# Second feed-forward block: gate row multiplied into all down weights, down sums added by DVE alone, four PSUM banks

## The chip, the cores and the metric

The kernel runs on one core of a Trainium2 chip. The metric is the device time of one execution in microseconds (us); the median of three runs of the kernel before is 2130.88 us (2127.46 to 2131.03). The five engines are named as in the profile: PE (TensorE, matrix products; PEld is its loading of weights), DVE (VectorE), ACT (ScalarE), POOL (GpSimd) and SP (SyncE, which here issues most DMAs).

## The reference, cut to what matters

The reference is a network of two layers on 512 latent tokens and 256 context tokens of 1024 features, all in float32. Each layer has a mixer and a gated feed-forward block, each followed by a layer norm. The change is in the feed-forward block of the second (last) layer, where only the 512 latent tokens are left:

```
def conv_ffn(h, rows, w_gate, w_up, w_conv, w_down):
    a = h @ w_gate
    a = dwconv2d_centred(a.reshape(bt, rows, lt // rows, D_FF), w_conv).reshape(bt, lt, D_FF)
    return (jax.nn.silu(a) * (h @ w_up)) @ w_down

x = layer_norm(DEEP_ALPHA * x + g_f * conv_ffn(hf, ...), ln_g[li, 1], ln_b[li, 1])
```

`D_FF` is 2816. `g_f` is the gate row: one factor for each of the 1024 output features, the same for all tokens. It multiplies the result of the down product, feature by feature, so multiplying each column of `w_down` by its factor gives the same sum.

## The kernel before, in words

Every float32 product is made from three products of halves: weights and activations are each split into a high part (`whi`, `hh`, rounded by a cast on ACT) and a low part (`wlo`, `hl`, the rest, by a subtraction on DVE or POOL; `split`, L139 to L148), and PE adds high times high, high times low and low times high in PSUM. All products go through line 115.

`ffn` (from L1362) is called once for each layer; `l` is the layer, and `key` is None in the second. The 2816 hidden features are taken in 11 steps `p` of 256. In each step `gate_up(p)` (L1407) loads two weight units of 1 MB (gate and up, L1409), splits them, and for each half of 128 features makes the products with gate (`g_ps`) and up (`u_ps`), 24 products of 512 columns each. ACT and DVE then make the 3x3 convolution from the gate sums (L1431, eight steps at L1442), the silu (L1453), the product with up (L1454) and the split into `hh` and `hl` (L1457).

One step later the down products of that hidden pair follow (L1482 to L1488). `unit_rows` (L190) loads 256 rows of the down weights (1 MB, L194), multiplies them by a row if one is given (two multiplications on POOL of 128x1024, L197), and splits them in four parts. For each of the four token tiles and each half of the 1024 output columns, `down` (L1379) makes six products into one PSUM bank (`d_ps`), DVE multiplies the sum by the gate row into `gt` (L1391), and `gt` is added to the running sum `acc` of the tile: by POOL for the first half of the columns, by DVE for the second (L1488). So a down block is 48 products in eight groups. The down sums of the loop have two PSUM banks (L1376); gate and up have two each. Nine units of down weights are used in the loop. The last two (L1494) get the gate row multiplied into the weights already, and their products come in the tail (L1500 to L1523) with four more banks (`dp2`, L1503); there DVE adds the bank straight to `acc`, and the layer norm and the output follow.

The raw weights pass through two buffers (`raw`, L281): a unit's DMA is issued by SP when the split of the unit two before it is done. The split halves of the second layer pass through four pairs of buffers (L1402), in the order down, gate, up of each step. The gate row is loaded in front of the loop (`gate_rows`, L1189; its addition on POOL is L1198). The running sums are scaled at L1471 (DVE) and get a bias row at L1491 (POOL).

The order of instructions on each engine is laid down when the program is built, by a planner that follows the order of the code and fills waits that it foresees with later work; so some gate products of the next step stand between the groups of a down block in the trace. `pin` (L150) keeps an instruction behind all that its engine was given so far.

Of the kernel before, what the change touches and what calls it, by code (L numbers as in the profile page):

```python
# [20 lines left out]
P = 128  # L21
# [76 lines left out]
class Net:  # L98
# [22 lines left out]
    def rsqrt(self, pool, x, n, mul, add, tag):  # L121
        """(x*mul + add)^-0.5 on [128, n] float32, by three Newton steps (each flips the sign) to full precision."""
        v = self.nc.vector
        hv = pool.tile([P, n], F32, tag=tag + "h", name="rs_h")
        y = pool.tile([P, n], F32, tag=tag + "y", name="rs_y")
        w = pool.tile([P, n], F32, tag=tag + "w", name="rs_w")
        v.tensor_scalar(out=hv, in0=x, scalar1=0.5 * mul, scalar2=0.5 * add, op0=ALU.mult, op1=ALU.add)
        v.tensor_scalar(out=y.bitcast(I32), in0=hv.bitcast(I32), scalar1=-0.5, scalar2=MAGIC,
                        op0=ALU.mult, op1=ALU.add)
        for _ in range(3):  # L130
            if n == 1:
                v.scalar_tensor_tensor(out=w, in0=y, scalar=hv[:, 0:1], in1=y, op0=ALU.mult, op1=ALU.mult)
            else:
                v.tensor_mul(w, y, y)
                v.tensor_mul(w, w, hv)
            v.scalar_tensor_tensor(out=y, in0=w, scalar=1.5, in1=y, op0=ALU.subtract, op1=ALU.mult)
        return y
# [12 lines left out]
    def pin(self, ins):  # L150
        """Queue an instruction behind all that its engine was given so far."""
        return self.tc.keep_in_program_order(ins)

    @contextmanager
    def priority(self, offset):
        """Emit with a priority shifted by offset (positive: later)."""
        tc = self.tc
        old = tc.cur_priority
        tc.cur_priority = max(0, old + offset)
        start = tc.cur_priority  # L160
        try:
            yield
        finally:
            tc.cur_priority = old + (tc.cur_priority - start)

    def hilo(self):
        """The two split halves of the next weight unit, from the open weight pools in turn."""
        ps = self.wps
        pool = ps[self.wcount % len(ps)]
        self.wcount += 1  # L170
        return (pool.tile([P, 8 * 256], F32R, tag="whi", name="whi"),
                pool.tile([P, 8 * 256], F32R, tag="wlo", name="wlo"))

    def unit(self, parts, scale=None):
        """Load weight columns (list of [1024, w] DRAM blocks), scaled if asked for, and split them: [128, 8, 256]."""
# [14 lines left out]
    def unit_rows(self, src, scale=None):  # L190
        """Load [256, 1024] weight rows, with columns scaled if given, and split them: [128, 2, 1024]."""
# [10 lines left out]
    def proj_fm_g(self, w, c0, dsts):  # L202
        """Feature-major products: dsts = [(psum [128, n], t0, n)]; weights stationary."""
        wh, wl = w
        xh, xl = self.hT
        for k in range(KT):
            for wi, xi, first, last in ((wh, xh, True, False), (wh, xl, False, False), (wl, xh, False, True)):
                for ps, t0, n in dsts:
                    self.mm(ps, wi[:, k, c0:c0 + P], xi[:, k, t0:t0 + n],
                            start=(k == 0 and first), stop=(k == KT - 1 and last))  # L210
                    yield n // 256

    def proj_tm_g(self, ps, w, t, c0=0, n=256):
        """Token-major products for token tile t; activations stationary."""
# [19 lines left out]
    def set_work(self, items, side=None):  # L234
        """items: [(weight parts, generator function of the loaded unit)], run in order by tick()."""
# [13 lines left out]
    def _step(self):  # L249
        """Advance the current item; its cost, or None at its end."""  # L250
# [19 lines left out]
    def drain(self, upto):  # L270
        """Run until the first `upto` items are complete."""
# [39 lines left out]
    def rows_T(self, pool, psp, src, n, dst, doff=0):  # L311
        """DRAM rows [n, 128] -> dst[:, doff:doff+n] (transposed)."""
# [7 lines left out]
    def cond(self, pool, psp):  # L320
        """silu(c), silu(c_ctx) as a zero-padded stationary operand [128, 8, 32]."""
# [22 lines left out]
    def mod_bias(self, pool, psp, l):  # L344
        """mod_b of layer l, per feature: [128, 48]."""
# [8 lines left out]
    def mod_group_g(self, mp, psp, l, g, tag="tr", bufs=2):  # L354
        """adaLN columns [2048 g, 2048 (g+1)) of layer l, both conditionings."""
# [30 lines left out]
    def h_params(self, key, lnidx, l, sub):  # L386
        """Scale/bias per feature of h = modulate(layer_norm(.)): from xhat."""
# [13 lines left out]
    def start(self, p2, w_in):  # L401
        """hT of layer 0, by pairs of feature tiles as the adaLN columns come in; q, k, v of delta heads."""
# [138 lines left out]
    def conv_evac(self, acc, blk, dst):  # L541
        """Three-tap convolution along the tokens of each stream, silu."""
# [120 lines left out]
    def fill_unit(self, fillp, pj, w, kind, i):  # L663
        """A 256-column block of the input projection, token-major, kept in DRAM."""
# [21 lines left out]
    def ab_load(self, w_in):  # L686
        """Columns 1792..2063: z of heads 2, 3 and the 16 decay / beta columns (one 272-column product)."""
# [13 lines left out]
    def ab_unit(self, dc, w_in):  # L701
# [5 lines left out]
        if True:  # L707
# [14 lines left out]
            # beta = 1 / (1 + exp(-b))  # L722
            nc.vector.tensor_scalar_add(be, e[:, 8:16], 1.0)
            nc.vector.reciprocal(be, be)
            # log1p(e) = 2 atanh(e / (2 + e))
# [17 lines left out]
        # decay columns: inclusive prefix, rest of the chunk, whole chunk  # L743
# [11 lines left out]
    def delta_head(self, h, hd, p1, p2):  # L755
# [3 lines left out]
        # norms  # L759
# [15 lines left out]
        bw = p2.tile([P, 2, 2, NT], F32, tag="bw", name="bw")  # (b, b * rest decay) x direction  # L775
# [6 lines left out]
        # decay matrices (transposed: row j, column i), products, U and P^T  # L782
# [38 lines left out]
    def delta_inverse(self, U, p1):  # L821
        """U_s = M_s^T, triangular, becomes ((I + M_s)^-1)^T: 16 x 16 by substitution, then block doubling."""
# [15 lines left out]
        # the 16 x 16 diagonal blocks, one per partition, each as a lower triangle: M (d = 0), M^T (d = 1)  # L838
# [29 lines left out]
        # 16 -> 32  # L868
# [16 lines left out]
        # 32 -> 64  # L885
# [37 lines left out]
        # 64 -> 128  # L923
# [19 lines left out]
    def delta_chain(self, h, hd, p1, p2):  # L943
# [65 lines left out]
        # rms_norm of (rq o), norm_w applied at the end  # L1009
# [13 lines left out]
    def ret_phase(self, st, accst, accp):  # L1023
# [34 lines left out]
        def finish(k):  # L1058
            """gate head k (delta heads, then retention heads), transpose and split: rows k of the output product."""
# [42 lines left out]
        # per head: load, state, output, normalise; the gated heads in between  # L1102
# [14 lines left out]
    def ret_head(self, h, hd, mask, rowd, cdec, p1, p2, trp, chp):  # L1117
# [17 lines left out]
        # state before each chunk, per direction  # L1135
# [28 lines left out]
        # group_norm  # L1164
# [24 lines left out]
    def gate_rows(self, pool, l, which, streams, gb=None):  # L1189
        """gate rows (per stream), broadcast over partitions."""  # L1190
# [11 lines left out]
    def affine_rows(self, pool, l, which):  # L1202
        """ln_g and ln_b of a layer norm, broadcast over partitions."""
# [30 lines left out]
    def ln_tile(self, r, st, xh, dst):  # L1234
        """r = alpha x + gate y with its statistics; xh = xhat, also written to dst (DRAM)."""
# [8 lines left out]
    def ln_out(self, r, st, rows, dst, spread):  # L1244
        """The normalised rows themselves, on DVE alone (shortest) or spread over ACT, DVE and Pool."""
# [19 lines left out]
    def h_tiles(self, key, tiles, xhs):  # L1265
        """hT[:, :, tiles] = modulate(LN) transposed, split."""
# [22 lines left out]
    def out_part(self, accs, units, k, last):  # L1289
        """Add feature tile k of the output product of two 256-column units to the open sums [(token tile, psum)]."""  # L1290
# [8 lines left out]
    def out_proj_ln(self, l, w_out, key, src, xh, groups, accp, accs, us, trp, gates=None):  # L1299
        """Output product and layer norm; accs: the sums of the first half of the columns."""  # L1300
        nc = self.nc
        with ExitStack() as st:
# [10 lines left out]
            else:  # L1313
                # the second half of the columns of w_out carries the gate already
# [47 lines left out]
    def ffn(self, l, has_ctx, acc, dst, key):  # L1362
# [10 lines left out]
        with ExitStack() as st0:  # L1373
            hidp = self.pool(st0, f"fhid{l}", bufs=2)
            lnp = self.pool(st0, f"lnF{l}")
            dp = self.pool(st0, f"ps_d{l}", bufs=2, space=PSUM)  # L1376
            hid = {}

            def down(w, x, t, n, ps, first=True, last=True, gated=False):  # L1379
                """Products of a hidden pair x = (hi, lo) with rows w for token tile t, half n."""  # L1380
# [13 lines left out]
            with ExitStack() as st:  # L1394
# [3 lines left out]
                if key:  # L1398
                    # the last two column units use wf and nextw
# [79 lines left out]
                for p in range(1, NP):  # L1479
                    if p > 1:  # L1480
                        gate_up(p)
                    if p < NP - 1:  # L1482
                        w, x = self.unit_rows(wd[(p - 1) * 256:p * 256, :]), hid.pop(p - 1)
                        for t in tiles:
                            for n in range(2):
                                ps = dp.tile([P, 512], F32, tag="d", name="d_ps")
                                o, gt = down(w, x, t, n, ps)
                                (v if n else g).tensor_add(o, o, gt)  # L1488
# [11 lines left out]
            with ExitStack() as st:  # L1500
                self.ln_pools(st, f"lnF{l}", ntr=2, side="right")
                gtp = self.ln2
                dp2 = self.pool(st, f"ps_dt{l}", bufs=4, space=PSUM)  # L1503
                dps = itertools.cycle((dp, dp2, dp2))
# [34 lines left out]
    def odd_mixer(self, acc_st):  # L1539
        nc, a = self.nc, self.a  # L1540
        v, g, s_ = nc.vector, nc.gpsimd, nc.scalar
        with ExitStack() as st0:
            y = self.hT
            pj = self.pool(st0, "ps_opj", bufs=2, space=PSUM)
            with ExitStack() as st:
# [24 lines left out]
                def rope(ps, t, out):  # L1570
                    """Two token tiles from t on."""
# [12 lines left out]
                def q_evac(q, ps, cs):  # L1584
                    """q = [hi of map 0, twice], [hi of map 1, twice], [lo of both], for two heads."""
# [7 lines left out]
                def k_evac(k, ps, cs):  # L1593
                    """k = [hi, lo of map 0], [lo, hi of map 1], for two heads."""
# [5 lines left out]
                def project(pr, passes, hd):  # L1600
                    """q, k, v of head pair pr into hd, by pairs of token tiles; yields between products."""
# [43 lines left out]
                def attend(h, q, k, vt, i):  # L1645
                    """Head h; yields after each query tile."""
# [3 lines left out]
                    for t in range(NLT):  # L1650
# [6 lines left out]
                        # the two maps' halves of the array work side by side  # L1657
# [16 lines left out]
                        # (p0 - lam (Z0 / Z1) p1); the common 1 / Z0 is applied to the sums  # L1674
# [139 lines left out]
```

## Time and profile before

| | before |
|---|---|
| median of three runs | 2130.88 us |
| span of the profiled execution, first to last instruction | 2123.7 us |
| PE busy, whole span | 1976.3 us (93%) |
| DVE busy | 1297.5 us (61%) |
| ACT busy | 703.5 us (33%) |
| POOL busy | 789.0 us (37%) |
| mean granted clock of PE | 0.971 |
| DMA bytes moved | 201.34 MB |

The profile is of one execution. A busy engine's time is the sum of its instructions; a PE that is busy is not always at its peak, since products are pipelined. Times in rows are counted from the start of the span. The granted clock is 1.00 when PE runs at 2.4 GHz. An arrow in brackets names what ended the idle time before an instruction. The second feed-forward block begins at about 1720 us and runs to the end.

### The profile page before, as it was taken

To read this page: it belongs to the slowest core of one execution; us is meant where nothing else is said; L and a number is where in the kernel's file an instruction comes from. 1 tells how busy PE (TensorE), PEld (TensorE's weight loads), DVE (VectorE), ACT (ScalarE), POOL (GpSimd) and SP (SyncE) were. 2 spreads that over 40 slices of the span, in tenths; PEclk is the share of its full clock that TensorE was granted. 3 is DMA by queue.
4 is the path that set the end of the run, shared out by engine and by line. 5 is a ranking of instruction groups with operands and counts; after the bars stand their busy time and mean duration, and the time that the engine had idled before them with its cause. 6 is when DMAs were issued, how large, how long until landed. Compare 5 with 4: busy or idle time off the path is not lost. (4 is left out here: it accounts for less than half of the span.)

```text
span 2123.7 us, 33676 instructions
## 1 busy us (share of the span) xinstructions
PE 1976.3 (93%) x13766; PEld 1676.6 (79%) x13766; DVE 1297.5 (61%) x2570; ACT 703.5 (33%) x1228; POOL 789.0 (37%) x430
## 2 busy tenths in 40 slices
PE   6989999999998999999999988988997989999997
PEld 4777777778898988888888868878886987777776
DVE  2354745544358675665555584566567787767676
ACT  2331343523344422222222243444444453222221
POOL 1233222212422344444444442212023135756582
PEclk8999999999999999999999999999997999999999
DMA  8536335465623311111111112100103142223221
GB/s 255 166 121 181 109 119 149 126 182 168 180 80 120 124 65 60 60 60 60 60 60 60 60 60 68 41 29 32 41 31 100 50 139 100 99 80 99 80 80 40
DMA packets 195586, 201.34 MB, mean 95 GB/s; under 512 B 21112, under 2 KB 183512, under 8 KB 195432
## 3 DMA queue, kind: packets, MB, share of 16 engines
q1 hardware_dynamic: 194136, 197.57, 29.2%
q8 instruction: 108, 1.77, 0.3%
q10 hardware_dynamic: 1296, 1.62, 0.3%
q14 instruction: 46, 0.38, 0.1%
HBM read 185.89 MB, written 13.27 MB: 94 GB/s over the span
## 5 line engine op out<-in xcount | busy, mean ns | idle before, releaser
L148 POOL TENSOR_TENSOR wlo<-raw,whi 128x2048 fp32r<-128x2048 f32 (+2 forms) x154 | 416.7, 2730 | 533.6 <-ACT whi L147 509.4
L1442 DVE SCALAR_TENSOR_TENSOR ac<-g_ps,fconvT,ac 128x441 f32<-128x441 f32 (+2 forms) x352 | 244.4, 694 | 190.9 <-ACT ac L1431 180.9
L147 ACT CAST whi<-raw 128x2048 fp32r<-128x2048 f32 (+2 forms) x177 | 200.4, 1169 | 393.5 <-PE d_ps L115 180.9
L115 PE MATMUL d_ps<-whi,hh 128*128 128x512 f32 x440 | 177.8, 404 | 21.1 <-DVE gt L1391 20.0
L115 PE MATMUL d_ps<-whi,hl 128*128 128x512 f32 x440 | 172.8, 393 | 0.6 <-DVE hl L148 0.6
L115 PE MATMUL d_ps<-wlo,hh 128*128 128x512 f32 x440 | 172.9, 393 | 0.0
L1488 POOL TENSOR_TENSOR acc<-acc,gt 128x512 f32<-128x512 f32 x90 | 129.7, 1450 | 69.4 <-DVE gt L1391 69.4
L115 PE MATMUL opj<-whi,hTh 128*128 128x256 f32 x512 | 151.6, 296 | 1.1 <-ACT oq L1591 1.1
L1391 DVE TENSOR_TENSOR gt<-d_ps,gate 128x512 f32<-128x512 f32 x192 | 130.6, 684 | 31.1 <-PE d_ps L115 28.9
L115 PE MATMUL opj<-whi,hTl 128*128 128x256 f32 x512 | 148.1, 289 | 0.0
L115 PE MATMUL opj<-wlo,hTh 128*128 128x256 f32 x512 | 147.9, 289 | 0.0
L115 PE MATMUL g_ps<-hTl,whi 128*128 128x512 f32 (+1 forms) x384 | 144.7, 377 | 1.1 <-POOL hTl L148 1.1
L115 PE MATMUL u_ps<-hTl,whi 128*128 128x512 f32 (+1 forms) x384 | 144.8, 377 | 0.2
L115 PE MATMUL u_ps<-hTh,wlo 128*128 128x512 f32 (+1 forms) x384 | 144.6, 377 | 0.0
L115 PE MATMUL u_ps<-hTh,whi 128*128 128x512 f32 (+1 forms) x384 | 144.5, 377 | 0.0
L115 PE MATMUL g_ps<-hTh,whi 128*128 128x512 f32 (+1 forms) x384 | 144.4, 376 | 0.0
L115 PE MATMUL g_ps<-hTh,wlo 128*128 128x512 f32 (+1 forms) x384 | 144.2, 376 | 0.0
L115 PE MATMUL fpj<-whi,hTh 128*128 128x256 f32 x432 | 126.9, 294 | 5.8 <-DVE kT L550 4.7
L115 PE MATMUL fpj<-wlo,hTh 128*128 128x256 f32 x432 | 126.9, 294 | 0.0
L115 PEld LDWEIGHTS d_ps<-whi,hh 128*128 128x128 f32 x440 | 83.0, 189 | 55.2 <-DVE gt L1391 38.9
L115 PE MATMUL fpj<-whi,hTl 128*128 128x256 f32 x432 | 126.0, 292 | 0.0
L115 PEld LDWEIGHTS opj<-whi,hTh 128*128 128x128 f32 x512 | 98.8, 193 | 7.2 <-issue 4.4
(464 smaller groups left out, 5014.8 us busy)
## 6 DMA issues: line engine op xcount, KB each, us to landing
mraw<-in_mod_w_dram SPq DMA_DIRECT2D x80, 512.0 KB
raw<-in_f_w_gate_dram SPq DMA_DIRECT2D x22, 1024.0 KB
raw<-in_f_w_up_dram SPq DMA_DIRECT2D x22, 1024.0 KB
raw<-in_f_w_down_dram SPq DMA_DIRECT2D x22, 1024.0 KB
raw<-in_o_w_qkv_dram SPq DMA_DIRECT2D x12, 1024.0 KB
raw<-in_e_w_in_dram SPq DMA_DIRECT2D x10, 1024.0 KB
mraw<-in_mod_w_dram SPq DMA_DIRECT2D x32, 256.0 KB
raw<-in_e_w_in_dram SPq DMA_DIRECT2D x12, 512.0 KB
```

The source lines that it names most:

```text
L115: self.nc.tensor.matmul(out, lhsT=lhsT, rhs=rhs, start=start, stop=stop)
L147: self.nc.scalar.copy(h, r)
L148: lo_eng.tensor_sub(l, r, h.bitcast(F32))
L1391: v.tensor_mul(gt, ps, gates[0 if t < NLT else 1][:, n * 512:(n + 1) * 512])
L1442: v.scalar_tensor_tensor(out=o, in0=pv[:, r0 + di:r1 + di, c0 + dj:c1 + dj], scalar=cw[(di + 1) * 3 + dj + 1], in1=o, op0=ALU.mult, op1=AL ...
L1488: (v if n else g).tensor_add(o, o, gt)
```

## The change

Four edits, all for the second layer alone (`has_ctx` is False and `key` is None there; the first layer's code stays as it was). The two pools of PSUM banks are shared out differently: four banks for the down sums of the loop instead of two, and in the tail two more instead of four, used in turn two to one. All nine units of down weights of the loop are loaded with the gate row. Their sums are added to `acc` straight from the bank, both halves by DVE. Comments are taken out elsewhere.

```
-            dp = self.pool(st0, f"ps_d{l}", bufs=2, space=PSUM)
+            dp = self.pool(st0, f"ps_d{l}", bufs=2 if has_ctx else 4, space=PSUM)
...
-                        w, x = self.unit_rows(wd[(p - 1) * 256:p * 256, :]), hid.pop(p - 1)
+                        w = self.unit_rows(wd[(p - 1) * 256:p * 256, :], None if key else gates[0])
+                        x = hid.pop(p - 1)
                         for t in tiles:
                             for n in range(2):
                                 ps = dp.tile([P, 512], F32, tag="d", name="d_ps")
-                                o, gt = down(w, x, t, n, ps)
-                                (v if n else g).tensor_add(o, o, gt)
+                                o, gt = down(w, x, t, n, ps, gated=not key)
+                                (v if n or not key else g).tensor_add(o, o, gt)
...
-                dp2 = self.pool(st, f"ps_dt{l}", bufs=4, space=PSUM)
-                dps = itertools.cycle((dp, dp2, dp2))
+                dp2 = self.pool(st, f"ps_dt{l}", bufs=4 if key else 2, space=PSUM)
+                dps = itertools.cycle((dp, dp2, dp2) if key else (dp, dp, dp2))
```

## Rows read from the trace of the kernel before

**Rows 1.** Stretches of the last block: time, busy time by engine (instructions), PEclk, DMA share, GB/s

```profile
1720.00:1768.00 48.00, 47.71 (x306) 42.58 (x305) 38.41 (x57) 27.30 (x36) 19.03 (x10) 1.00 0.45 154
...
1785.00:1806.00 21.00, 21.00 (x92) 16.92 (x91) 11.32 (x17) 6.34 (x8) 9.16 (x3) 1.00 0.14 51
1911.00:1924.40 13.40, 12.06 (x53) 9.32 (x52) 12.48 (x16) 3.31 (x6) 10.94 (x9) 1.00 0.49 157
...
2051.60:2068.20 16.60, 14.21 (x54) 10.91 (x53) 14.27 (x17) 3.60 (x7) 16.60 (x11) 0.90 0.18 64
```

**Rows 2.** Waits, 1700 to 2124 us: total us, times, longest us

```profile
ACT whi L147 <- PE d_ps L115: 59.0, 9, 9.2
...
PEld d_ps L115 <- DVE gt L1391: 21.9, 18, 2.7
...
PE d_ps L115 <- DVE gt L1391: 13.3, 13, 2.2
```

**Rows 3.** Chain that ended last, 1690 to 2124 us: start, us, engine, tile, count

```profile
1924.53 4.90 PE g_ps L115 x21
1929.44 5.60 PE u_ps L115 x24
...
1959.73 4.90 PE g_ps L115 x21
...
2030.08 4.90 PE g_ps L115 x21
...
2067.95 4.90 PE g_ps L115 x21
...
2089.65 6.84 PE d_ps L115 x30
```

**Rows 4.** Timeline of PE: start, us, instruction

```profile
1768.97 0.40 PE L115 MATMUL d_ps<-whi,hh 128*128 128x512 f32 x1
...
1784.04 0.40 PE L115 MATMUL g_ps<-hTh,wlo 128*128 128x512 f32 x1
...
1910.87 0.40 PE L115 MATMUL d_ps<-whi,hh 128*128 128x512 f32 x1
...
1916.09 0.39 PE L115 MATMUL d_ps<-whi,hl 128*128 128x512 f32 x1
```

**Rows 5.** Groups by line, 1700 to 2124 us, shapes apart

```profile
L1488 POOL TENSOR_TENSOR acc<-acc,gt 128x512 f32<-128x512 f32 x36 | 50.1, 1401 | 21.5 <-DVE gt L1391 21.5
L1391 DVE TENSOR_TENSOR gt<-d_ps,gate 128x512 f32<-128x512 f32 x72 | 48.4, 682 | 9.0 <-PE d_ps L115 7.8 <-POOL acc L1488 1.2
L1488 DVE TENSOR_TENSOR acc<-acc,gt 128x512 f32<-128x512 f32 x36 | 45.5, 1263 | 0.6
...
L197 POOL TENSOR_TENSOR raw<-raw,gate 128x1024 f32<-128x1024 f32 x4 | 10.8, 2726 | 5.0 <-DMA raw<-in_f_w_down_dram 5.0
...
L1523 DVE TENSOR_TENSOR acc<-acc,d_ps 128x512 f32<-128x512 f32 x8 | 5.5, 682 | 3.1 <-PE d_ps L115 3.1
```

**Rows 6.** Instructions on tile gt, 1750 to 2124 us: ns min/median/max

```profile
L1391 DVE TENSOR_TENSOR gt<-d_ps,gate x72: 673/678/692, 1773.3 to 2068.0; 128x512 f32<-128x512 f32 x72
...
L1488 DVE TENSOR_TENSOR acc<-acc,gt x36: 691/1228/2856, 1775.7 to 2068.7; 128x512 f32<-128x512 f32 x36
```

**Rows 7.** Timeline of DVE in one down block

```profile
1907.80 4.38 DVE L1442 SCALAR_TENSOR_TENSOR ac<-g_ps,fconvT,ac 128x441 f32<-128x441 f32 x6 [4.18 <-ACT ac L1431]
...
1918.09 1.06 DVE L148 TENSOR_TENSOR hl<-ac,hh 128x512 fp32r<-128x512 f32 x1
```

**Rows 8.** Timeline of POOL, first block and ninth

```profile
1739.10 2.40 POOL L1198 TENSOR_TENSOR gate<-gate,raw 128x1024 f32<-128x1024 f32 x1 [6.58 <-issue]
1746.17 10.12 POOL L148 TENSOR_TENSOR wlo<-raw,whi 128x512 fp32r<-128x512 f32 x5 [4.66 <-ACT whi L147]
...
2041.77 5.22 POOL L197 TENSOR_TENSOR raw<-raw,gate 128x1024 f32<-128x1024 f32 x2 [5.03 <-DMA raw<-in_f_w_down_dram]
2048.01 10.09 POOL L148 TENSOR_TENSOR wlo<-raw,whi 128x2048 fp32r<-128x2048 f32 x5 [1.03 <-ACT whi L147]
```

## The prediction

> **What bounds the kernel now.** I read the stretches of time first, since the change touches only the last feed-forward block (1720 to 2124 us of the span). In 1785 to 1806 us, products of gate and up alone, PE is busy all the time at a granted clock of 1.00. In 1911 to 1924.4 us, which is one down block (the 48 products of one unit of down weights), it is busy 12.06 of 13.40 us, and DVE 12.48. In 2051.6 to 2068.2 us, the last down block of the loop, it is busy 14.21 of 16.60, POOL the whole 16.60, and the clock falls to 0.90 [rows 1]. So PE is the bound, but it stops in each down block. The waits say for what: PE and its weight loads wait for DVE's gt, the multiplication that frees a down bank, in 18 places, two for each of nine blocks [rows 2]. ACT's wait for PE in the same answer (59.0 us) is a buffer waiting to be freed, thus work that came early, not late [rows 2].
>
> How much time that is comes from the chain. From the start of the gate products behind one down block to the same point a round later it is 1959.73 - 1924.53 = 35.20 us [rows 3]. The round holds 96 products of gate and up, 24 of them in 5.60 us [rows 3], so 22.40 us; and 48 down products. The first and the 24th of an undisturbed run of those start at 1910.87 and 1916.09, 23 steps of 0.227 us [rows 4], so 10.90 us. The round could take 33.30 us: 1.90 are lost. There are seven such blocks (second to eighth), 13.3 us. Behind the ninth the step in the chain is 2067.95 - 2030.08 = 37.87 us [rows 3], 4.57 lost, lowered clock included. In the first block 15.07 us pass from the first down product to the gate product behind the last [rows 4]; 48 down and five gate products in between need 12.06, so 3.0 are lost. Together **20.9 us** is the most that the loop can give back.
>
> **What the change does, part by part.**
>
> DVE. It removes 72 multiplications of 682 ns and 36 additions of 1263 ns, and adds 72 additions that read the down bank, for which the same instruction stands in the tail: 682 ns [rows 5]. Per block 10.5 us become 5.5. Could the new addition be stretched beside POOL, as the old one was (691 to 2856 ns)? The multiplication, which like it reads one operand from the bank and one from SBUF, lasted 673 to 692 ns in all 72 cases, with POOL at work beside many [rows 6]. I take 682, the nearest row; the upper bound is 1263. The Trainium skill (SBUF — State Buffer, section Who interferes with whom) has a rule on this: a DVE instruction contends with GpSimd when both of its inputs are in SBUF, and not with at most one. The traces agree, and by this rule the sum stands at 5.5 us per block; without it it would be 10.1. The same rule speaks against the change in one place: the new multiplications on POOL can stretch DVE's split of the hidden values, which has two inputs in SBUF. At the longest of such rows, 2.9 us [rows 6], that would be 1.8 us more for the split in a block, and the additions do not wait for it unless the order says so (rival A).
>
> Does DVE then keep up? In the block of [rows 7] its convolution starts at 1907.80. Eight steps of 0.73 us (4.38 for six), the product with up, the split of 1.06 us and eight additions come to 5.8 + 0.7 + 1.1 + 5.5 = 13.1 us, so 1921 at the earliest. PE, unhindered, ends the block at 1910.87 + 10.90 = 1921.8. With four banks PE needs the k-th addition only when group k + 4 begins; the first must be done 5.4 us after the block starts, at 1916.3, and by then DVE needs only the convolution and one addition (1914.3). Even at 1263 ns the fourth addition would be done about 1920.5, where group eight begins at 1920.4. So the wait vanishes at either bound.
>
> Banks. Four down banks instead of two fill the eight (gate two, up two). That the four let PE run on shows in the tail, which has its own four: 30 down products in 6.84 us, 0.228 each [rows 3], against 0.227 undisturbed, so 0.03 us lost in five groups. In the tail the change shares out the same six banks differently (four and two), and each of the eight sums still finds one freed long before: I cost it at nothing, covered by four groups of 1.36 us. At the block's start gate and up get other banks than now, which the last output sums and transposes leave. PE is busy 47.71 of 48.00 us there [rows 1]: at most 0.3 to gain. A bank that is freed late would cost what PE finds no other product for; I bound it by one run of 24, 5.6 us [rows 3], once. I take 0, as the nearest row is PE's full time there.
>
> POOL. It loses 36 additions (50.1 us) and gains 18 multiplications of 128x1024 at 2726 ns (49.1 us) [rows 5]: no load either way, but the work moves from behind the products to ahead of them. Per unit, 5.45 us now stand between the landing of the down weights and ACT's cast. Behind the waiting multiplication on POOL's queue stands the split of the next up weights, and behind ACT's cast the silu of the block. What it costs is shown by the ninth unit of the trace, which carries its gate already: the multiplication waits 5.03 us for the DMA, runs 2041.77 to 2046.99, and the split of the up weights starts at 2048.01 all the same, having waited 1.03 us for ACT [rows 8]. The cover is thus the time in which POOL waits for ACT's next cast, 1.03 us to spare. Should it go, the up weights' split is late by what is missing, at most 5.45 us; those weights are used behind a whole run of gate products of 5.60 us, and only in the next round. The number of DMAs and their queue don't change. In the first block the gate row is ready at 1741.5, the first split of down weights starts at 1746.17 [rows 8], and the first down product at 1768.97 [rows 4]; 5.45 us more on a path with over 15 us of room. At nothing, at most 0.5 in this block. The tenth unit's multiplication now stands in POOL's way in the ninth block; with no additions on POOL, nothing of PE's waits for it.
>
> **The sum.** 20.9 less what a block may still lose, 0.15 each (the tail shows 0.03 for five groups, five times that as a margin), 1.4: **19.5 us**. The span is 2123.7 us, 7.2 below the median of the runs (2130.88), and I take these 7.2 as unchanged: 2104.2 + 7.2 = 2111.4.
>
> **Rivals.**
>
> A. The order, not the load, holds PE. Instructions of an engine run in the order that was planned for them; if DVE's first addition stands behind the split of the hidden values (five steps later in the chain DVE, ACT, DVE, ACT, DVE, about 1916.8 in the block of [rows 7]), it is done at 1917.5, and the fifth group waits 1.2 to 1.4 us. For: DVE's order of now has such places. Against: the multiplications of now stand between the steps of the convolution. It gives 20.9 - 9 x 1.4 = 8.3 us: 2122.6. Chance 0.14.
>
> B. Nothing that counts: the stops go on in the same length under another name, because the planned order of PE keeps gate products and a late bank between the down groups. 2130.9. Against it speaks that each wait has DVE's gt at its end [rows 2]. Chance 0.04.
>
> C. Slower: the two raw buffers become the bound. Three units a round (gate, up, down) pass through two of them, each held from its DMA until its split is done, so 2 x 35.2 = 70.4 us of holding a round. If none of that were waiting, 5.45 us more would make the round 37.9, and nine rounds cost 9 x 2.7 = 24 us: 2155. It decides from the point where the hold is work alone. Against it: ACT's waits for PE of 59.0 us [rows 2] are holds without work, and the ninth unit changed nothing in its round [rows 8]. Chance 0.05.
>
> Forecast (the loop's waits go): 0.77, within 2107.5 and 2115. The lower end is the whole 20.9, the 0.3 at the start and the spread of the runs (2127.5 to 2131.0). To hold 8 in 10 the range reaches into rival A, to 2120. A difference of 0.2%, 4.3 us, is what a measurement of this kernel can tell from none. Faster by more: the forecast and nearly all of A, 0.90; within: B and the rest of A, 0.05; slower: C, 0.05.
>
> **What would show it.** Right: no idle time of PE with a DVE releaser in the down blocks; rounds of 33.3 to 33.5 us in the chain; down products in one unbroken run of 48; the granted clock 1.00 between 2050 and 2070; 72 additions on DVE near 682 ns; POOL's busy time about as before; 22 multiplications at L197. Wrong: rounds above 34.5 with PE waiting for DVE's addition (A); PE waiting for POOL's split, or a down DMA issued later in the round than now (C).

## The result: 12 us faster, and the profile after

The changed kernel takes 2113.01 us (median of six runs, 2102.70 to 2122.62), the kernel before 2125.32 us beside it (six runs, 2119.79 to 2131.03). The ratio is 0.9943, with a 95% interval of 0.9923 to 0.9962: by the ratio a gain of 12.1 us, between 8 and 16 (12.3 by the two medians).

The two profiled executions differ by more, 2123.7 - 2100.9 = 22.8 us of span. Ten of these lie ahead of the changed code: the first gate or up product of the block stands at 1720.50 us before and at 1710.50 after, and already the first down products of the first layer, whose code is the same, start at 762.5 and 755.8. That part varies: in the twelve profiled executions of this document the product stands between 1710.5 and 1723.6 us. So from here on I measure each kernel from that product to the end of its span, and call it **the layer's block**: 403.20 us before, 390.40 after, 12.8 less, in line with the timed runs.

Stretches of the changed kernel; columns as in [rows 1]. The first line is the start, the second the first down block, then the gate and up products behind it, the second down block and the ninth.

```profile
1710.00:1760.50 50.50, 48.69 (x310) 43.23 (x308) 38.37 (x53) 26.18 (x34) 23.82 (x12) 1.00 0.43 147
1760.50:1778.00 17.50, 12.94 (x51) 10.30 (x50) 16.76 (x21) 4.59 (x8) 12.44 (x7) 0.90 0.38 121
1778.00:1800.00 22.00, 22.00 (x95) 17.68 (x95) 12.41 (x15) 6.35 (x6) 12.80 (x4) 1.00 0.15 48
1800.20:1811.30 11.10, 11.10 (x50) 9.16 (x49) 10.22 (x13) 3.44 (x6) 8.40 (x6) 1.00 0.60 189
2033.30:2044.40 11.10, 11.10 (x51) 9.16 (x50) 8.65 (x13) 3.44 (x6) 10.41 (x7) 1.00 0.29 96
```

In the second and the ninth block PE no longer stops (11.10 of 11.10 us; before, 12.06 of 13.40 in the middle and 14.21 of 16.60 in the ninth [rows 1]), and the clock of the ninth is 1.00, not 0.90. But the first block has become worse: 12.94 us busy of 17.50, and the low clock now stands there.

The chain of the changed kernel, as in [rows 3]:

```profile
1748.93 8.38 DVE acc L1471 x4
...
1763.67 4.45 DVE hl L148
...
1770.26 0.60 DVE acc L1489
1770.91 7.09 PE d_ps L115 x24
1778.00 5.60 PE g_ps L115 x24
...
1800.40 10.90 PE d_ps L115 x48
1811.31 5.60 PE g_ps L115 x24
...
1844.61 5.60 PE g_ps L115 x24
...
2033.55 10.91 PE d_ps L115 x48
...
2066.85 6.84 PE d_ps L115 x30
```

A round is now 1844.61 - 1811.31 = 33.30 us, where it was 35.20, and each down block from the second on is one unbroken run of 48 products in 10.90. Ahead of 1770.91, where PE goes on in the first block, the chain runs through DVE: four scalings of `acc` (L1471) in 8.38 us, a split of hidden values in 4.45. Waits of the changed kernel in its last 400 us, columns as in [rows 2]:

```profile
PEld d_ps L115 <- DVE acc L1489: 5.0, 1, 5.0
PE d_ps L115 <- DVE acc L1489: 4.6, 1, 4.6
...
PEld g_ps L115 <- POOL hTl L148: 2.4, 3, 0.9
PE g_ps L115 <- POOL hTl L148: 1.8, 3, 0.7
```

The waits of PE for DVE in 18 places [rows 2] are down to one, of nearly 5 us, and a small one at the start of the block is new. Two groups of DVE, shapes apart, in the same stretch, columns as in [rows 5]:

```profile
L148 DVE TENSOR_TENSOR hl<-ac,hh 128x512 fp32r<-128x512 f32 x22 | 34.9, 1586 | 8.3 <-ACT hh L147 7.9
...
L1471 DVE TENSOR_TENSOR acc<-acc,lng 128x1024 f32<-128x1024 f32 x4 | 8.5, 2170 | 0.0
```

Before, the same 22 splits took 22.2 us (mean 1007 ns), and the four scalings 4.6 (1214 ns). **The ledger** of the layer's block, in us, is thus: start (first product to first down product) 48.47 before, 50.23 after, +1.8; loss of the first block (its length up to the second less 33.30) 3.0 before, 6.2 after, +3.2; seven middle blocks 7 x 1.90 = -13.3; the ninth -4.6. Together -12.9, against 12.8 measured. Every kernel below is read by the same ledger.

### The profile page after: what moved, and what is told of

Its sections match the earlier page's. It is cut to its first block, busy times and chain, and to the rows that moved or that the text cites. A ratio compares the mean times of both kernels' runs of the same rounds, so it can differ in the third digit from the quotient of the medians.

```text
span 2100.9 us, 33593 instructions
## 1 busy us (share of the span) xinstructions
PE 1961.3 (93%) x13766; PEld 1668.8 (79%) x13766; DVE 1272.7 (61%) x2534; ACT 703.8 (33%) x1228; POOL 777.8 (37%) x412
## 3 DMA queue, kind: packets, MB, share of 16 engines
q8 instruction: 108, 1.77, 0.4%
## 5 line engine op out<-in xcount | busy, mean ns | idle before, releaser
L115 PEld LDWEIGHTS opj<-whi,hTl 128*128 128x128 f32 x512 | 98.3, 192 | 2.8 <-issue 2.4
L115 PEld LDWEIGHTS opj<-wlo,hTh 128*128 128x128 f32 x512 | 98.5, 192 | 2.3 <-issue 1.2
```

The lines of the kernel that those rows point to most:

```text
L115: self.nc.tensor.matmul(out, lhsT=lhsT, rhs=rhs, start=start, stop=stop)
```

## The experiments

Questions: which of the two parts, banks or gate folded into the weights, empties the blocks, where the 3 us more in the first block come from, and what makes the start 1.8 us longer. L numbers are those of the kernel the edit starts from.

**Banks alone (e1).** On the kernel before, only the shares of the banks:

```
-            dp = self.pool(st0, f"ps_d{l}", bufs=2, space=PSUM)
+            dp = self.pool(st0, f"ps_d{l}", bufs=2 if has_ctx else 4, space=PSUM)
...
-                dp2 = self.pool(st, f"ps_dt{l}", bufs=4, space=PSUM)
-                dps = itertools.cycle((dp, dp2, dp2))
+                dp2 = self.pool(st, f"ps_dt{l}", bufs=4 if key else 2, space=PSUM)
+                dps = itertools.cycle((dp, dp2, dp2) if key else (dp, dp, dp2))
```

> The kernel before with the two bank edits alone: multiplication by the gate row and additions stay as they were. Theory (the banks set the wait): DVE has 25 us of work in a round, so with four banks PE need not wait for it; rounds of 33.3 to 33.5 us in the seven middle blocks, with only the ninth block still losing about 1 to 2 us, and the whole block of the layer some 14 to 17 us shorter than before. Rival (DVE's load in the down block sets it: 10.5 us of multiplications and additions beside 7.9 us of convolution and split in 10.9 us): rounds stay above 34.5 us.

Layer's block 385.33 us, 17.9 less than before and 5.1 less than the whole change; start 50.24, loss of the first block 1.1, of all others none. That is more than the 14 to 17 us expected, since the ninth block loses nothing either. The waits and the chain of this kernel:

```profile
PEld d_ps L115 <- DVE gt L1391: 1.2, 1, 1.2
```

```profile
1798.57 10.90 PE d_ps L115 x48
...
1831.87 10.91 PE d_ps L115 x48
```

And a stretch of one round of it, the down block and the 22.40 us behind, columns as above:

```profile
1798.57:1809.47 10.90, 10.90 (x49) 9.01 (x49) 10.36 (x14) 3.29 (x6) 9.67 (x8) 1.00 0.61 192
1809.47:1831.87 22.40, 22.40 (x98) 18.03 (x97) 13.94 (x20) 6.50 (x7) 13.35 (x5) 1.00 0.14 48
```

DVE still does multiplication and addition, and has 24.30 of 33.30 us of work in the round. With two banks PE had to take its stops inside the block; with four DVE falls behind and makes it up beside gate and up. So it was not DVE's load over the round that held PE; with the load of before in the down block, two banks were too few.

**Gate folded in alone (e2).** On the changed kernel, the banks as before:

```
-            dp = self.pool(st0, f"ps_d{l}", bufs=2 if has_ctx else 4, space=PSUM)
+            dp = self.pool(st0, f"ps_d{l}", bufs=2, space=PSUM)
...
-                dp2 = self.pool(st, f"ps_dt{l}", bufs=4 if key else 2, space=PSUM)
-                dps = itertools.cycle((dp, dp2, dp2) if key else (dp, dp, dp2))
+                dp2 = self.pool(st, f"ps_dt{l}", bufs=4, space=PSUM)
+                dps = itertools.cycle((dp, dp2, dp2))
```

> The changed kernel with two down banks in the loop and four more in the tail, as before: gate row in the weights and 72 additions on DVE stay. Theory (the banks set the wait): DVE's convolution stands between the additions, so with two banks some 0.3 to 1 us per block is still lost, rounds of 33.6 to 34.4 us. Rival (DVE's load sets it): rounds of 33.3 us with two banks too. In the first block, both: a wait of 4 to 7 us, since DVE comes late there.

Layer's block 395.16 us, 8.0 less than before; start 48.50. Six of the middle blocks run unbroken in 10.90, so here the lighter load of DVE is enough with two banks: the rival came true in these, and not the 0.3 to 1 us per block of the theory. But 9.4 us are lost in the first block, 1.5 in the second and 1.8 in the ninth. Waits and chain:

```profile
PEld d_ps L115 <- DVE acc L1489: 10.7, 3, 7.2
```

```profile
1819.81 0.68 DVE ac L1454
1820.49 0.68 DVE acc L1489
1821.18 2.54 DVE hl L148
1824.38 3.02 PE d_ps L115 x12
...
1849.80 10.91 PE d_ps L115 x48
```

In the second block a split of hidden values of 2.54 us stands on DVE ahead of the addition that PE waits for (in the first one of 3.99, in the ninth one of 2.82): the mechanism of rival A, which with two banks decides in three blocks. So either part alone empties most of the blocks; together they do the same work twice, and the folding costs 5 us (390.40 against 385.33).

**The first unit without the gate (e3), the first two (e3b).** Theory: in the first steps the new multiplications on POOL (L197) delay POOL's splits, and these then run beside DVE instructions with two inputs in SBUF. In the changed kernel, timeline of POOL, then of DVE (start, us, instruction):

```profile
1737.51 4.79 POOL L197 TENSOR_TENSOR raw<-raw,gate 128x1024 f32<-128x1024 f32 x2 [2.71 <-DVE ac L1442]
...
1747.74 5.08 POOL L148 TENSOR_TENSOR wlo<-raw,whi 128x2048 fp32r<-128x2048 f32 x1
...
1758.24 4.78 POOL L197 TENSOR_TENSOR raw<-raw,gate 128x1024 f32<-128x1024 f32 x2 [5.42 <-DMA raw<-in_f_w_down_dram]
...
1762.96 4.61 POOL L148 TENSOR_TENSOR wlo<-raw,whi 128x2048 fp32r<-128x2048 f32 x1
```

```profile
1748.86 5.05 DVE L1471 TENSOR_TENSOR acc<-acc,lng 128x1024 f32<-128x1024 f32 x1
...
1763.67 4.45 DVE L148 TENSOR_TENSOR hl<-ac,hh 128x512 fp32r<-128x512 f32 x1
```

The first scaling starts at 1748.86 and ends at 1753.91, 1.09 us behind the end of POOL's split (1752.82); alone it lasts 1.21. The split of hidden values ends at 1768.12, 0.55 behind POOL's (1767.57); at its shortest it lasts 0.69. In both, the time until POOL is done is added to nearly the whole of the instruction's own. The same sum holds in every kernel of this document: 17 instructions of the last block (this scaling and 16 splits of hidden values, in twelve traces) begin while POOL is in a split of 128x2048, and each lasts what is then left of POOL's instruction plus its own 1.21 or 0.69 us, less 0.13 to 0.15. The kernel before has the collision too, in its first down block (timeline of DVE, then of POOL):

```profile
1767.68 2.88 DVE L148 TENSOR_TENSOR hl<-ac,hh 128x512 fp32r<-128x512 f32 x1
...
1765.38 4.63 POOL L148 TENSOR_TENSOR wlo<-raw,whi 128x2048 fp32r<-128x2048 f32 x1 [9.08 <-ACT whi L147]
```

So the change did not bring it in, it made it longer. In e3 and e3b the first unit, or two, keep the old way:

```
-                        w = self.unit_rows(wd[(p - 1) * 256:p * 256, :], None if key else gates[0])
+                        w = self.unit_rows(wd[(p - 1) * 256:p * 256, :], None if key or p <= 1 else gates[0])
...
-                                o, gt = down(w, x, t, n, ps, gated=not key)
-                                (v if n or not key else g).tensor_add(o, o, gt)
+                                o, gt = down(w, x, t, n, ps, gated=not key and p > 1)
+                                (v if n or not key and p > 1 else g).tensor_add(o, o, gt)
```

(in e3b with 2 for 1).

> The changed kernel, but the first of the nine units is loaded without the gate row, its sums multiplied by it on DVE and added by POOL and DVE as before. Theory (the multiplication on POOL moves POOL's split of the first weights onto DVE's scaling of the running sums, both read SBUF with two inputs, and DVE comes late to the first block): the four scalings take 4.5 to 5.5 us in place of 8.4, the wait of PE in the first block falls from 4.6 us to under 1.5, the layer's block is 4 to 6 us shorter than in the changed kernel. Rival (the order planned for DVE sets it, the first addition stands behind the split of the hidden values): the wait of 4 to 5 us stays.

> The changed kernel, but the first two of the nine units without the gate row, their sums multiplied on DVE and added as before. With one unit plain the multiplication of the second unit fell into DVE's scaling of the running sums (9.06 us for four, and 4.8 us without a product on PE). Theory (two engines reading SBUF with two inputs each): with no multiplication on POOL in that stretch the four scalings take 4.6 us, the first block loses at most 1.2 us, and the layer's block takes 384.5 to 385.8 us, like the one with the banks alone (385.3). Rival (the order planned for DVE): the first block still loses over 3 us.

e3 lost 5.9 us in its first block (layer's block 390.09), hardly less than the whole change with 6.2; PE's stop there is 3.96 us. e3b lost 1.0 (385.22), as its theory said. The rows of the scalings (ns min/median/max), first e3:

```profile
L1471 DVE TENSOR_TENSOR acc<-acc,lng x4: 1217/2322/3442, 1760.6 to 1766.2; 128x1024 f32<-128x1024 f32 x4
```

e3b:

```profile
L1471 DVE TENSOR_TENSOR acc<-acc,lng x4: 1212/1216/1217, 1761.6 to 1765.0; 128x1024 f32<-128x1024 f32 x4
```

In e3 it is now the second unit's multiplication that meets them, and it pays as well (timeline of POOL in e3; the pair took 4.78 above):

```profile
1762.58 6.01 POOL L197 TENSOR_TENSOR raw<-raw,gate 128x1024 f32<-128x1024 f32 x2 [5.12 <-DMA raw<-in_f_w_down_dram]
```

So e3 missed its numbers, and by PE's wait alone it came out as its rival said; the rows above show why, and e3b, where the order rival would have kept a loss of over 3 us, decides against it. What counts is whether a POOL instruction runs when DVE comes to its scalings and splits, not which unit it belongs to.

**Multiplication cut short (e4).** In the changed kernel the multiplication covers 8 columns of each half, so that POOL's queue keeps its order and loses nearly all of the time (the kernel leaves out most of the gate, and serves only to read the time):

```
-                nc.gpsimd.tensor_mul(raw[:, k * D:(k + 1) * D], raw[:, k * D:(k + 1) * D], scale)
+                nc.gpsimd.tensor_mul(raw[:, k * D:k * D + 8], raw[:, k * D:k * D + 8], scale[:, :8])
```

> The changed kernel with the multiplications on POOL cut to the first 8 of 1024 columns: so most of the gate is left out, and what the multiplications cost is seen. Theory: rounds stay at 33.3 us (the multiplications are covered there); the first block's wait falls from 4.6 us to under 1.5, as POOL's splits end before DVE's scaling. Rival (order): nothing changes but POOL's busy time, about 55 us less. A third case, that the multiplications cost something in each round, would show as rounds below 33.3.

Layer's block 384.21 us, loss of the first block 0.0; no wait of PE for DVE is left in the block, and the first run of 48 is whole (chain):

```profile
1767.69 10.91 PE d_ps L115 x48
```

In the layer's block PE and POOL run the same instructions in the same order as in the changed kernel, and so does DVE but for one step of a convolution; the split ahead of the first addition lasts 0.69 us here, not 4.45. The 6.2 us of the first block thus hang on POOL's time in those multiplications, with banks and additions of the change in place.

**POOL's split in four pieces (e9).** If a DVE instruction waits for the POOL instruction that is running, shorter ones must shorten the single wait. In the changed kernel the gate and up units are split in four parts, as the down units are (L1474):

```
-                self.cparts = 1
+                self.cparts = 1 if key else 4
```

> The whole change, with the low halves of gate's and up's weights split on POOL in four pieces of 128x512 instead of one of 128x2048, as the down weights are. Theory (a DVE instruction with two inputs in SBUF waits until the one POOL instruction that is running has ended: 5.05 us for one scaling beside a piece of 5.08 us, 4.45 us for the split of the hidden values beside one of 4.61 us): no scaling and no split of hidden values in the first two steps takes over 3 us, PE's wait in the first block falls from 4.6 to under 2.5 us, and the layer's block takes 386 to 388 us. Rival (DVE is slowed by POOL's load, not by the length of its instructions): the wait stays at 4 us or more.

Layer's block 386.33 us, loss 2.1. The scalings in this kernel:

```profile
L1471 DVE TENSOR_TENSOR acc<-acc,lng x4: 1739/2312/2318, 1756.0 to 1762.1; 128x1024 f32<-128x1024 f32 x4
```

None lasts longer than 2.32 us. The third begins at 1759.87, when 1.24 us are left of POOL's piece, and lasts these and its own 1.21 less 0.14; POOL's piece is stretched in turn (timeline of DVE, then of POOL, then of both at the split of hidden values):

```profile
1759.87 2.31 DVE L1471 TENSOR_TENSOR acc<-acc,lng 128x1024 f32<-128x1024 f32 x1
...
1758.83 2.28 POOL L148 TENSOR_TENSOR wlo<-raw,whi 128x512 fp32r<-128x512 f32 x1
...
1771.30 2.30 DVE L148 TENSOR_TENSOR hl<-ac,hh 128x512 fp32r<-128x512 f32 x1
...
1770.66 2.40 POOL L197 TENSOR_TENSOR raw<-raw,gate 128x1024 f32<-128x1024 f32 x1 [5.07 <-DMA raw<-in_f_w_down_dram]
```

All four scalings together still take 8.4, as in the changed kernel, since each now meets a piece. What is saved is the split of hidden values right ahead of the first addition, 2.30 us in place of 4.45, and PE's stop falls from 4.6 to 1.8. But that split meets a multiplication by the gate row here, not a piece, so part of the gain is one of phase. The theory holds, since in both places the wait ends with the one POOL instruction that is running; "four pieces are free of the collision" would be too much.

**Three banks (e5).** In the changed kernel:

```
-            dp = self.pool(st0, f"ps_d{l}", bufs=2 if has_ctx else 4, space=PSUM)
+            dp = self.pool(st0, f"ps_d{l}", bufs=2 if has_ctx else 3, space=PSUM)
...
-                dp2 = self.pool(st, f"ps_dt{l}", bufs=4 if key else 2, space=PSUM)
-                dps = itertools.cycle((dp, dp2, dp2) if key else (dp, dp, dp2))
+                dp2 = self.pool(st, f"ps_dt{l}", bufs=4 if key else 3, space=PSUM)
+                dps = itertools.cycle((dp, dp2, dp2) if key else (dp, dp2))
```

> The changed kernel with three down banks in the loop (three more in the tail, in turn). Theory: rounds of 33.3 us, as with four; in the first block, where DVE is late, PE runs one group less ahead and waits 1.2 to 1.5 us longer than the changed kernel's 4.6. Rival (four are needed in each block): some rounds above 33.4 us. At the start of the layer the gate products come to another bank again: 48.4 to 50.3 us from the first product to the first down product, either is possible.

Layer's block 386.34: start 48.02, loss of the first block 4.0, second block 11.05 us, then 10.91, the ninth 11.12. With the gate folded in, three banks do for the rounds (0.15 and 0.2 us lost). The first block missed its number: its scalings were not held (1206 to 1209 ns), the split ahead of the first addition lasted 3.36 us, and PE's stop was 2.1 us, not more than 4.6. Which instructions meet depends on a few microseconds of phase, which each edit moves; a single wait of this kind cannot be forecast by adding to another kernel's.

**Two more banks, placed apart (e6), and e1 with more runs (e7).** In e1 and in the change the start is 1.8 us longer, in e2 not. e6 leaves the pools of the kernel before and opens two more banks for the down sums behind those of gate and up, which so keep their places:

```
+                dpx = dp if has_ctx else self.pool(st, f"ps_dx{l}", bufs=2, space=PSUM)
+                dpl = itertools.cycle((dp, dpx))
...
-                                ps = dp.tile([P, 512], F32, tag="d", name="d_ps")
+                                ps = next(dpl).tile([P, 512], F32, tag="d", name="d_ps")
```

> The kernel before with two more down banks for the loop, but behind the banks of gate and up instead of in front of them, so that gate and up keep the banks that they had; gate row, multiplications and additions as before. Theory (moving gate and up to other banks cost 1.8 us at the layer's start): 48.5 us from the first product to the first down product instead of 50.2, rounds of 33.3, about 1 us lost in the first block; the layer's block takes 383.5 to 384.0 us against 403.2 before, so about 0.9% of the time is gained (ratio 0.989 to 0.993). Rival (the 1.8 us come from the run, not the banks): 50.2 stays.

> The kernel before with the two bank edits alone, now timed. By its profile the layer's block takes 385.3 us against 403.2 before and 390.4 with the whole change: ratio 0.990 to 0.994, about 5 us under the whole change. Rival (the multiplication of the weights pays after all): not under the whole change's 0.994.

e6: 2104.79 us (median of six, 2101.33 to 2110.01), ratio 0.9908 [0.9890, 0.9926]. e7: 2105.05 us (2100.77 to 2114.93), ratio 0.9920 [0.9898, 0.9943]; the kernel before beside them 2124.75 (eleven runs, 2118.53 to 2132.96). Layer's block 383.98 and 385.17; start 48.46 and 50.22; loss of the first block 1.5 and 1.0. The waits at the start of e6:

```profile
PEld u_ps L115 <- POOL hTl L148: 0.6, 2, 0.3
```

In the kernels with moved banks the gate products come first, and their weight loads wait for POOL's `hTl` 2.4 us in three places (the third wait of the changed kernel above), PE itself 1.8. In the kernel before and in e6 up's products come first. So the start's 1.8 us come from which banks gate and up get, with the other order of products that comes with them. e6 has the shortest layer's block of the kernels that compute the whole result; by their timed runs e6 and e7 cannot be told apart. e6 beats the kernel before by 20 us, and the change by about 8 (20.0 less 12.3, each against the kernel before beside it; the layer's blocks are 6.4 apart), with DVE's and POOL's work left as it was.

**The change with banks apart (e8).** The whole change with e6's way to get the banks: e2's edit, and e6's two additions and the line in the loop.

> The whole change, but with the two added down banks behind those of gate and up, which so keep their old banks (the tail's banks as before). Theory (the start's 1.8 us come from the move of gate and up, the first block's loss from the multiplications on POOL, and the two are independent): 48.5 us from the first product to the first down product instead of 50.2, rounds of 33.3 us, and still 4 to 6.5 us lost in the first block, so the layer's block takes 388 to 389 us against 390.4. Rival (the loss of the first block hangs on the start): the first block loses under 2 us.

Layer's block 386.92 us: start 48.48, loss of the first block 4.4. The start goes back as in e6 while the first block still loses, so the two costs are separate, though not wholly independent: the loss is 4.4 and not 6.2, and the block is 1 to 2 us shorter than expected. Folding costs 386.92 - 383.98 = 2.9 us here and 5.1 in the other arrangement. Here the scalings were not held (1209 to 1215 ns), but two splits of hidden values lasted 3.70 and 4.05 us, and PE's stop was 2.6.

The ledger of all kernels, in us:

| kernel | layer's block | start | loss, 1st block | loss, other blocks |
|---|---|---|---|---|
| before | 403.20 | 48.47 | 3.0 | 17.9 |
| the change | 390.40 | 50.23 | 6.2 | 0 |
| e1 banks alone | 385.33 | 50.24 | 1.1 | 0 |
| e7 the same, timed | 385.17 | 50.22 | 1.0 | 0 |
| e6 banks apart | 383.98 | 48.46 | 1.5 | 0 |
| e2 gate alone | 395.16 | 48.50 | 9.4 | 3.3 |
| e8 change, banks apart | 386.92 | 48.48 | 4.4 | 0 |
| e3 first unit plain | 390.09 | 50.25 | 5.9 | 0 |
| e3b two plain | 385.22 | 50.24 | 1.0 | 0 |
| e4 multiplication short | 384.21 | 50.23 | 0.0 | 0 |
| e5 three banks | 386.34 | 48.02 | 4.0 | 0.3 |
| e9 split in four | 386.33 | 50.24 | 2.1 | 0 |

The layer's block less start and losses is 334.0 us in every line, to 0.2: nothing else in the block moved.

## Why the prediction was right, and where it was not

The time came out right (2111.4 forecast, 2113.0 measured), and inside the forecast's own range. The saving did not: 19.5 us were forecast, 12 to 13 came. The two agree because the base moved the other way: the forecast stood on a median of 2130.88, and over six runs the kernel before has 2125.32, 5.6 less. That the time was met so closely is luck; that the eight later blocks were emptied is not. By the ledger the shortfall is 19.5 - 12.8 = 6.7 us: 6.1 in the first block and 1.8 at the start, less 1.2 of reserve that the other eight blocks did not need.

- **"PE is the bound, but it stops in each down block", 20.9 us in all: right.** e6, which empties all blocks but the first, gains 19.2 us, which is 20.9 less the 1.5 still lost in its first block, to 0.2.
- **Seven blocks of 1.90 and the ninth of 4.57: right**, all 17.9 us came back. The 0.15 per block kept in reserve was not needed; the rounds are 33.30.
- **The additions at 682 ns: right.** Tile `d_ps` in the changed kernel:

```profile
L1489 DVE TENSOR_TENSOR acc<-acc,d_ps x72: 673/687/689, 1770.2 to 2044.5; 128x512 f32<-128x512 f32 x72
```

  Not one of 72 is stretched, though POOL is at work beside many; with one input in the bank they don't meet it.
- **POOL in the first block, "5.45 us more on a path with over 15 us of room. At nothing, at most 0.5 in this block": the step that failed.** The block lost 6.2 us in place of the 0.15 forecast, and with it failed the sign "no idle time of PE with a DVE releaser in the down blocks". The room was real: the down weights were there in time. What I did not follow is what POOL's shifted work runs beside. I had the rule in hand (the Trainium skill, SBUF — State Buffer, section Who interferes with whom) and priced it at 1.8 us for one split of hidden values, by the longest row of before; the four scalings of L1471, in front of the same block, were not counted, and neither was that such an instruction is held for all that is left of POOL's: 5.05 us for a scaling that ends 1.09 us behind a POOL split. The Trainium skill (SBUF — State Buffer, section Summary: rules for kernel authors) says so too: with two SBUF inputs against a GpSimd instruction that reads SBUF, the second one to issue is blocked until the first finishes. The traces agree, by the 17 instructions above. And "the additions do not wait for it unless the order says so": here the order says so, since the first addition stands behind that split on DVE (1763.67, then 1770.26 in the chain).
- **"Does DVE then keep up?": right for the second to the ninth block, whose pattern is that of [rows 7]; wrong for the first**, to which I applied it without looking. There DVE has the scalings ahead of it, comes to its first addition at 1770.26, and PE had finished its four groups (24 products) by then.
- **"At the block's start gate and up get other banks ... I take 0": failed by 1.8 us**, inside the bound of 5.6 that was named. e6 and e8 show it as the move of the banks.
- **The tail at nothing: right**, 30 down products in 6.84 us in both [rows 3].
- **Rival A** (the order holds the fifth group in each block) did not come in the blocks from the second on; its mechanism is what happens in the first block. B and C did not come: the two raw buffers carry the 5 us without a longer round, and L197's waits for its DMA (47.3 us in ten places) show that POOL is ahead of the weights there.
- **That both parts are needed was never said, but the sum was made as if they were one.** The text priced DVE's load and the banks separately and did not ask whether one would do. [rows 1] held the answer: DVE busy 12.48 of 13.40 us in the down block, but 11.32 of 21.00 behind it, so it had room to make up what two banks would not let it put off.

## What to carry to other kernels

Where an engine that empties PSUM is full inside one stage and half idle in the next, try more banks before less work: two banks alone gave 20 us here, and the folding of the gate on top of them took 3 to 5 back. Work moved to POOL shifts everything behind it on POOL's queue, so list the DVE instructions with two SBUF inputs near the new places, the one-time ones ahead of a loop too, and price each at its own time and what may be left of the POOL instruction beside it, at most the whole. Price the first round of a loop by its own rows, and when a pool of banks changes size, look at which later pools get other banks.

## What was not expected of the hardware

- The wait for POOL does not show as a wait. It lies inside the duration of the DVE instruction (1.21 us alone, 5.05 beside a POOL split of 5.08), so the list of waits has no line for it, and only minimum and maximum of a group give it away. POOL is stretched too: its pair of multiplications took 4.78 us alone and 6.01 beside the scalings.
- A stop of PE can cost more than its length. Stretches of the changed kernel around the stop, columns as above:

```profile
1766.00:1770.90 4.90, 0.34 (x2) 0.00 (x0) 4.83 (x6) 0.00 (x0) 4.90 (x4) 0.95 0.41 120
1770.90:1774.00 3.10, 3.09 (x8) 2.48 (x9) 3.10 (x6) 0.10 (x1) 2.04 (x2) 0.53 0.47 157
1774.00:1778.00 4.00, 4.00 (x19) 3.31 (x18) 3.58 (x6) 1.16 (x2) 0.00 (x0) 1.00 0.82 262
```

  Behind the stop the granted clock is 0.53 for 3.1 us, thus nearly all of it at the lower level of 1.2 GHz, and the 24 products take 7.09 us in the chain where half of a whole block takes 5.45. Of the 6.2 us lost, about 4.7 are the stop (from 0.23 behind the start of the last product at 1765.96 to 1770.91) and 1.5 the clock. Not every stop does this: in e9, after an idle time of 1.77 us, the clock stayed at 1.00, and so it did in the first block of the kernel before, after 2.21; in e5 a stop of 2.1 us was followed by 3.1 us at 0.68 and 3.6 at 0.80. So the length of the stop alone does not decide it, and what else does is not shown here.
